# One layer step on one core: TensorE's order in projection, gates and branch products, from a planner's to the program's

## The chip, the cores and the metric

The kernel runs on one core of a Trainium2 chip. The metric is the device time of one execution in microseconds; the kernel before was run three times. TensorE (called PE in the profile) does matrix products and transposes into PSUM; ScalarE (ACT) and VectorE (DVE) read PSUM and do everything elementwise; GpSimd (POOL) does a part of the elementwise work in SBUF; SyncE (SP) issues nearly all DMAs.

## The reference

One inference step of a backbone of two layers over 384 tokens (128 context tokens and 256 latent ones) with 1024 channels. Each layer has a token mixer and an MLP; the change lies in the mixer:

```python
p = _project(h, lp)                        # h @ w_in: inputs of four mixers, and 4 x 1024 gates
o_a = _dense_attention(...)                # A: latent attention, 4 heads
o_b, s_f, s_b = _bi_retention(...)         # B: retention in both directions, 4 heads
o_c = _banded_attention(...)               # C: window and sink, 4 query heads, 2 key heads
o_d = _dense_attention(...)                # D: normalised q and k, 4 query heads, 2 key heads
terms = [jax.nn.sigmoid(gates[..., i * D_MODEL:(i + 1) * D_MODEL]) * (o @ lp['w_branch'][i])
         for i, o in enumerate(outs)]
y = (terms[0] + terms[1] + terms[2] + terms[3]) @ lp['w_o']
x = _layernorm(ALPHA * x + g1 * y, lp['ln1_g'], lp['ln1_b'])
h = x * (1 + sc2) + sh2
f = jnp.square(jax.nn.relu(h @ lp['w_up'])) @ lp['w_down']
x = _layernorm(ALPHA * x + g2 * f, lp['ln2_g'], lp['ln2_b'])
```

## The kernel before

**Precision and products.** Every large product is done as three matmuls: both operands are split into a high and a low part, and high by high, high by low and low by high are summed in PSUM (`mm3`, lines 119 to 122). So lines L120, L121 and L122 are the tile products in all rows; the attention's small matmuls and all transposes have lines of their own (L680 scores, L718 transposes of the softmax, L736 values, L899 transposes of q and k, L809 to L845 branch A's preparation, L965 to L1086 branch B).

**Stages of a layer's mixer.** The projection (lines 1135 to 1142) goes over chunks of columns. A chunk of the kinds a, c, d and b2 gives three tiles, one per block of 128 tokens, each of 24 matmuls with 256 columns (`proj`, L653); a chunk of the kind qk gives two tiles of 24 matmuls with 384 columns (`qk_b`, L945). Layer 0 has six chunks here (16 tiles), layer 1 eight (22 tiles). Then come the four branches in the order A, C, D, B, called br 0, 2, 3, 1 in the code (lines 1193 to 1208). Each has eight gate tiles of 24 matmuls with 384 columns (`gates`, L1148), and after each two gate tiles two branch products of six matmuls with 384 columns each (`products`, L1159), which read a finished branch's output.

**The step.** After each projection or gate tile the program calls `tick()` (L465), and this runs one step of a software pipeline (class `Pipe`, L416). Its 31 tasks, added in lines 1096 to 1122, start one per step, and each task does its next stage in each later step. A task of attention has the stages scores, turn and values (L674, L712, L727): scores are TensorE's product, then the row maximum on VectorE (L689), the negated maximum (L697, or L693 in C), the exponential on ScalarE (L700), the reciprocal (L705) and the scaling (L707 and L708); turn transposes the result; values multiplies it with V. Four such tasks for each of A, C and D alternate between a batch of two query blocks (eight score matmul records) and one of a single block (four). Stages that are marked late (turn) come last in a step. In program order the first scores of A stand in step 6 and their turn in step 7; C's first scores stand in step 14, right behind the transposes of C's last block that they read, and their turn in step 15; C's third batch has its scores in step 18 and its turn in step 19; D's first batch has them in steps 21 and 22. All steps from 1 to 34 have work for TensorE; later ones have none. A step also may take VectorE work of the conditioning's linear map from a list (`ada_v`, L370).

**What sets the order.** The framework traces the program and then a planner orders each engine's instructions by its own estimate of when inputs are ready, with program order as priority. The helper `behind` (L129) adds an edge that fixes the order of two instructions of one engine, without a semaphore; `in_order` (L156) puts such edges between all instructions of the named engines in a block, so that the planner has no choice there. Before, it stands around the first product and around the ends of the two other large products. In `Pipe.step` the helper `held` keeps a step's work behind what was last issued two steps earlier (`HOLD = 2`). In projection, gates and branch products nothing else fixes TensorE's order.

**Buffers that matter.** PSUM has the pools `psa` (three banks: scores take two per batch, and branch products one each), `psg` (two: tiles of projection and gates), `psm` (two: transposes) and `pso` (one). Weights come by SyncE's DMAs into six raw buffers, and ScalarE and VectorE split each into `wh` and `wl` (L281 and L125), four buffers deep.

Of the kernel before, what the change touches and what calls it, by code (L numbers as in the profile page):

```python
# [50 lines left out]
BR_ORDER = (0, 2, 3, 1)  # L51
# [42 lines left out]
def kernel(ctx, tc, a):  # L94
# [14 lines left out]
    def nm(s):  # L109
        counter[0] += 1  # L110
        return f"{s}_{counter[0]}"

    def bank(pool):
        return pool.tile([P, 512], F32, tag="bank", name=nm("bank"))
# [4 lines left out]
    def mm3(out, a_hl, b_hl, start, stop):  # L119
        mm(out, lhsT=a_hl[0], rhs=b_hl[0], start=start, stop=False)  # L120
        mm(out, lhsT=a_hl[0], rhs=b_hl[1], start=False, stop=False)  # L121
        mm(out, lhsT=a_hl[1], rhs=b_hl[0], start=False, stop=stop)  # L122
# [6 lines left out]
    def behind(later, earlier):  # L129
        tc.add_manual_dep(later, earlier.name,  # L130
                          mybir.DependencyInfo(mybir.DependencyClass.NoSync, mybir.DependencyReason.DATA),
                          reason="issue order")
# [22 lines left out]
    @contextmanager  # L155
    def in_order(engines=COMPUTE):  # L156

        pinned.clear()
        n = len(nc.cur_bb.bb.instructions)
        yield  # L160
        for i in nc.cur_bb.bb.instructions[n:]:
            if i.engine in engines and "DMA" not in type(i).__name__:
                if i.engine in pinned:
                    behind(i, pinned[i.engine])
                pinned[i.engine] = i

    def view(hl, pattern, **kw):
        return tuple(t.rearrange(pattern, **kw) for t in hl)
# [57 lines left out]
    def cond_rows(alloc):  # L226
        nc.sync.dma_start(out=csr, in_=a["cond"].partition_broadcast(P))
        for c in range(2):
            for h in range(2):
                x, th = csr[:, c, h * 512:(h + 1) * 512], alloc()  # L230
                nc.scalar.activation(th, x, AF.Tanh, scale=0.5)
                nc.vector.tensor_scalar(out=th, in0=th, scalar1=0.5, scalar2=0.5, op0=ALU.mult, op1=ALU.add)
                nc.vector.tensor_tensor(out=x, in0=x, in1=th, op=ALU.mult)
# [4 lines left out]
    class Stream:  # L238
# [21 lines left out]
        def next(self, splits=SPLITS_AHEAD):  # L260
            i = self.at
            self.at += 1
            self.split(i)
            self.ahead(splits)
            return self.sub[i]
# [19 lines left out]
    def by_k(subs, k):  # L285

        out = []
        for hl in subs:
            v = view(hl, "p (k n) -> p k n", k=k)
            out += [(v[0][:, i], v[1][:, i]) for i in range(k)]  # L290
        return out

    stream = Stream()
    n_f = D_FF // P
    nq = 0
    for l in range(L):
# [14 lines left out]
        for k in range(n_f):  # L311
            f = k + AHEAD if k < n_f - REST else n_f
# [99 lines left out]
    def hk(k):  # L412
        return tuple(h[:, k, :] for h in hT)


    class Pipe:  # L416
# [10 lines left out]
        def step(self):  # L427
            if self.tasks:
                self.live.append(self.tasks.pop(0))
            self.marks.append(last_issued())  # L430
            marks = self.marks[-HOLD - 1] if len(self.marks) > HOLD else {}
            stages = [t.pop(0) for t in self.live if t]
            for late in (False, True):
                for f in stages:
                    if getattr(f, "late", False) == late:
                        with held(marks):
                            f()
            self.live = [t for t in self.live if t]
# [19 lines left out]
    for l in range(L):  # L458
        last = l == L - 1
        pipe = Pipe()  # L460
        p2 = None
# [3 lines left out]
        def tick():  # L465
            pipe.step()
            ticks[0] += 1
            n = 2 if p2 else ([0] + [c for f, c in TICK_OPS if f <= ticks[0]])[-1]
            for _ in range((n + ticks[0] % 2) // 2):
                next(ada_v, None)  # L470
# [130 lines left out]
        at_ctx = tc.tile_pool(name=f"attn{l}", bufs=1, reuse_waits="tile")  # L601
        at = at_ctx.__enter__()

        def t2(name):
            return at.tile([P, 512], F32, tag="t2", name=nm(name), bufs=T2N)
# [22 lines left out]
        def evac_to(key, c0, scale=None):  # L628
            def f(t, b, n=256):
                if (key, t) not in tm:  # L630
                    tm[key, t] = t2("tm" + key)
                x = tm[key, t][:, c0:c0 + n]
                if scale is None:
                    nc.scalar.copy(x, b[:, :n])  # L634
                else:
                    nc.scalar.mul(x, b[:, :n], scale)
            return f

        def proj_part(b, w, n, t, k0, k1):
            for k in range(k0, k1):  # L640
                mm3(b[:, :n], hcol(k, t), w[k], k == 0, k == KT - 1)
# [11 lines left out]
        def proj(w, n, evac, step):  # L653
            for t in range(3):
                b = bank(psg)
                proj_part(b, w, n, t, 0, KT)
                evac(t, b)
                step()
# [286 lines left out]
        def qk_b(i0, scale):  # L945

            def f(w, i):
                if i0 + i == 0:
                    bt["qk"] = at.tile([P, 4, NTOK], F32, tag="kb", name=nm("qkB"))
                b = bank(psg)  # L950
                for k in range(KT):
                    mm3(b[:, :NTOK], tuple(q[:, i * P:(i + 1) * P] for q in w[k]), hk(k), k == 0, k == KT - 1)
                if scale is None:
                    nc.scalar.copy(bt["qk"][:, i0 + i, :], b[:, :NTOK])
                else:
                    nc.scalar.mul(bt["qk"][:, i0 + i, :], b[:, :NTOK], scale)
            return f
# [167 lines left out]
        chunks = [("d", 0, None), ("d", 256, None), ("qk", 0, None), ("qk", 2, 0.125), ("b2", 0, None), ("b2", 256, 0.5)]  # L1125
# [3 lines left out]
        else:  # L1129
            chunks = [("c", 0, None), ("c", 256, None)] + chunks  # L1130
        for t in range(3):
            evac_to("a", 0)(t, banks_a[t], A_W)
        if l == 0:
            cond_rows(lambda: t2("acc"))
        for key, c0, scale in chunks:
            w = by_k([stream.next(), stream.next()], 4)
            if key == "qk":
                for i in range(2):
                    qk_b(c0, scale)(w, i)
                    tick()  # L1140
            else:
                proj(w, 256, evac_to(key, c0, scale), tick)


        acc = [None] * KT
# [2 lines left out]
        def gates(ts_):  # L1148
            for _ in range(2):
                w = view(stream.next(), "p (k n) -> p k n", k=KT)  # L1150
                b = bank(psg)
                for k in range(KT):
                    mm3(b[:, :NTOK], (w[0][:, k], w[1][:, k]), hk(k), k == 0, k == KT - 1)
                tt = t1.tile([P, NTOK], F32, tag="T1", name=nm("tt"), bufs=T1N)
                nc.scalar.activation(tt, b[:, :NTOK], AF.Tanh, scale=0.5)
                ts_.append(tt)
                tick()

        def products(br, c0, ts_, done, hl):  # L1159
            w = view(hl, "p (k n) -> p k n", k=2)  # L1160
            while not o_done[br]:
                tick()
            for i in range(2):
                cc = c0 % 4 + i
                b = bank(psa)
                for k in range(2):
                    mm3(b[:, :NTOK], (w[0][:, k, cc * P:(cc + 1) * P], w[1][:, k, cc * P:(cc + 1) * P]),
                        (o_hl[br][0][:, k], o_hl[br][1][:, k]), k == 0, k == 1)
                done(c0 + i, ts_[i], b[:, :NTOK])
# [20 lines left out]
                                           op1=ALU.subtract)  # L1190
            mT[c] = (mh, ml)

        for n, br in enumerate(BR_ORDER):
            done = (first_done, mid_done, mid_done, last_done)[n]
            for half in range(2):
                if n == 3 and half == 0:
                    while pipe.busy():
                        tick()
                    at_ctx.__exit__(None, None, None)
                    p2_ctx = tc.tile_pool(name=f"p2_{l}", bufs=1, reuse_waits="tile")  # L1200
                    p2 = p2_ctx.__enter__()
                hl = None
                for c0 in (4 * half, 4 * half + 2):
                    ts_ = []
                    gates(ts_)
                    if hl is None:
                        hl = stream.next()
                    products(br, c0, ts_, done, hl)

        def lnc_tile():  # L1210
            return p2.tile([P, D], F32, tag="lnc", name=nm("lnc"), bufs=4)
# [490 lines left out]
```

## Time and profile before

| | us |
|---|---|
| median of 3 runs | 1277.07 |
| lowest and highest | 1276.08, 1277.44 |
| profiled execution, its time | 1276.65 |
| span of its profile | 1274.5 |
| TensorE busy in it | 1253.8 |
| VectorE, ScalarE, GpSimd busy | 854.1, 583.5, 211.2 |

Busy time of TensorE counts a matmul until its modelled end, so consecutive matmuls overlap; what one of a stream costs is the distance between two starts. The rows that the prediction uses come from the page's first part (busy time by engine), from the view by windows (busy time of each engine in chosen stretches) and from the timeline of one engine.

### The profile page before, as it was taken

Reading aid. Unit: us, or ns where it says so; the run is one execution under the profiler, and the core shown is the slowest. Engines: PE = TensorE matmul, PEld = TensorE weight load, DVE = VectorE, ACT = ScalarE, POOL = GpSimd, SP = SyncE. Lnnn points to the kernel's source line nnn. Section 1 sums busy time; section 2 is a strip of 40 time slices with the busy share of each in tenths; the row PEclk is TensorE's granted clock in tenths of the full one; section 3 lists DMA queues with packets and bytes.
Section 4 is the critical chain, followed back from the end, with each engine's and each line's share of the span. In section 5 each row is a group of like instructions: output and inputs, shape, how many; then the busy total and the mean of one; then the engine's idle time right before and its main releaser. Section 6 shows DMA issues by size and latency. Waiting matters only on the chain. (4 is left out here: it accounts for less than half of the span.)

```text
span 1274.5 us, 19089 instructions
## 1 busy us (share of the span) xinstructions
PE 1253.8 (98%) x7246; PEld 1137.6 (89%) x7246; DVE 854.1 (67%) x1537; ACT 583.5 (46%) x1051; POOL 211.2 (17%) x214
## 2 busy tenths in 40 slices
PE   9999999999999999999999999999999999999996
PEld 6789888999989999999898988999998999999995
DVE  4676875899779999343586876597456893333336
ACT  4564564333545444454365566233343744444442
POOL 0031200333232000000061210024221500000003
PEclk9999999999999999999999999999999999999998
DMA  9843323459627887453223422348344263334421
GB/s 366 330 154 118 123 100 104 145 197 337 226 83 246 269 271 273 149 176 140 102 98 133 158 92 83 121 155 322 119 148 162 109 209 132 125 124 159 165 74 50
DMA packets 64827, 211.65 MB, mean 166 GB/s; under 512 B 9248, under 2 KB 13536, under 8 KB 64608
## 3 DMA queue, kind: packets, MB, share of 16 engines
q1 hardware_dynamic: 62016, 201.49, 45.3%
q0 software_dynamic: 2432, 8.42, 2.0%
q8 instruction: 57, 0.93, 0.3%
q10 hardware_dynamic: 288, 0.52, 0.1%
q14 instruction: 34, 0.28, 0.1%
HBM read 206.28 MB, written 4.13 MB: 165 GB/s over the span
## 5 line engine op out<-in xcount | busy, mean ns | idle before, releaser
L125 DVE TENSOR_TENSOR wl<-raw,wh 128x1024 fp32r<-128x1024 f32 (+1 forms) x251 | 317.6, 1270 | 299.4 <-ACT wh L281 298.8
L281 ACT CAST wh<-raw 128x1024 fp32r<-128x1024 f32 x249 | 260.5, 1050 | 447.7 <-PE bank L121 286.9
L120 PE MATMUL bank<-hTh,wh 128*128 128x384 f32 x1040 | 351.4, 338 | 0.0
L122 PE MATMUL bank<-hTh,wl 128*128 128x384 f32 x1040 | 348.8, 336 | 0.6 <-DVE wl L125 0.6
L121 PE MATMUL bank<-hTl,wh 128*128 128x384 f32 x1040 | 348.5, 335 | 0.0
L120 PEld LDWEIGHTS bank<-hTh,wh 128*128 128x128 f32 x1040 | 195.3, 188 | 5.0 <-issue 1.9
L121 PEld LDWEIGHTS bank<-hTl,wh 128*128 128x128 f32 x1040 | 195.3, 188 | 3.2 <-issue 0.9
L122 PEld LDWEIGHTS bank<-hTh,wl 128*128 128x128 f32 x1040 | 195.2, 188 | 1.2 <-DVE wl L125 0.9
L121 PE MATMUL bank<-wl,uh 128*128 128x512 f32 x384 | 150.4, 392 | 0.0
L122 PE MATMUL bank<-wh,ul 128*128 128x512 f32 x384 | 150.3, 392 | 0.0
L120 PE MATMUL bank<-wh,uh 128*128 128x512 f32 x384 | 149.6, 390 | 0.0
L370 DVE CUSTOM_DVE_ANT_0 acc<-raw,csr,bT 128x1024 bf16<-128x1024 f32 x80 | 105.0, 1327 | 1.7 <-POOL rope L756 0.9
L370 DVE CUSTOM_DVE_ANT_0 acc<-lnc,csr,bT 128x1024 bf16<-128x1024 f32 x80 | 100.5, 1293 | 0.0
L1183 POOL TENSOR_TENSOR tt<-tt,tt 128x384 f32<-128x384 f32 x48 | 65.5, 1382 | 205.5 <-DVE tt L1182 205.5
L122 PEld LDWEIGHTS bank<-wh,ul 128*128 128x128 f32 x384 | 71.9, 188 | 15.4 <-DVE ul L125 0.4
L120 PEld LDWEIGHTS bank<-wh,uh 128*128 128x128 f32 x384 | 72.1, 188 | 13.9
L121 PEld LDWEIGHTS bank<-wl,uh 128*128 128x128 f32 x384 | 72.1, 188 | 13.9
L120 PE MATMUL bank<-wh,hTh 128*128 128x256 f32 x240 | 71.7, 299 | 0.2 <-ACT tmc L634 0.2
L122 PE MATMUL bank<-wh,hTl 128*128 128x256 f32 x240 | 68.7, 286 | 0.0
L121 PE MATMUL bank<-wl,hTh 128*128 128x256 f32 x240 | 68.3, 285 | 0.0
L391 POOL DMA_DIRECT2D gd<-gs x4 | 2.4, 595 | 290.4 <-DMA raw<-in_w_u_dram 158.0
L700 ACT ACTIVATE p<-bank,neg 128x384 f32<-128x384 f32 (+1 forms) x72 | 35.8, 508 | 30.1 <-DVE neg L697 16.2
(273 smaller groups left out, 1824.6 us busy)
## 6 DMA issues: line engine op xcount, KB each, us to landing
raw<-in_w_g_dram SPq DMA_DIRECT2D x64, 512.0 KB, 3.5
raw<-in_w_d_dram SPq DMA_DIRECT2D x64, 512.0 KB, 3.5
raw<-in_w_u_dram SPq DMA_DIRECT2D x58, 512.0 KB, 3.6
raw<-in_w_av_dram SPq DMA_DIRECT2D x40, 512.0 KB, 3.9
lnc<-in_w_av_dram SPq DMA_DIRECT2D x40, 512.0 KB, 4.5
raw<-in_w_q_dram SPq DMA_DIRECT2D x28, 512.0 KB, 3.9
raw<-in_w_ada_dram SPq DMA_DIRECT2D x16, 512.0 KB, 8.4
raw<-in_w_b_dram SPq DMA_DIRECT2D x16, 512.0 KB, 3.7
```

The costliest lines, as they stand in the source:

```text
L120: mm(out, lhsT=a_hl[0], rhs=b_hl[0], start=start, stop=False)
L121: mm(out, lhsT=a_hl[0], rhs=b_hl[1], start=False, stop=False)
L122: mm(out, lhsT=a_hl[1], rhs=b_hl[0], start=False, stop=stop)
L125: nc.vector.tensor_tensor(out=low, in0=x, in1=high.bitcast(F32), op=ALU.subtract)
L281: nc.scalar.copy(wh, raw)
L370: nc.vector.tensor_tensor_reduce(out=alloc().bitcast(BF16), in0=w, in1=csr[:, c], scale=1.0, scalar=bT[:, l, u, b:b + 1], op0=ALU.mult, op ...
L391: nc.gpsimd.dma_start(out=g_dram[l][w].rearrange("c (k p) -> (c k) p", p=P), in_=gs)
L700: nc.scalar.activation(p[:, j, c], ss[j][:, c], AF.Exp, bias=neg[:, i, j:j + 1], scale=scale, accum_out=su[:, i, j:j + 1])
L1183: nc.gpsimd.tensor_tensor(out=acc[c], in0=acc[c], in1=t_, op=ALU.add)
```

## The change

TensorE's instructions of the two loops are put between edges of `in_order`, the first block around the projection's chunks, the second around the four branches with gates and products; steps that `tick` runs inside are part of the block. Only TensorE's order is fixed: a tile's 24 matmuls, then all of that step's TensorE work in program order, then the next tile or the branch products. No instruction is added or taken away, and the order of the other engines stays with the planner.

```diff
-        for key, c0, scale in chunks:
-            w = by_k([stream.next(), stream.next()], 4)
-            if key == "qk":
-                for i in range(2):
-                    qk_b(c0, scale)(w, i)
-                    tick()
-            else:
-                proj(w, 256, evac_to(key, c0, scale), tick)
+        with in_order((mybir.EngineType.PE,)):
+            for key, c0, scale in chunks:
+                w = by_k([stream.next(), stream.next()], 4)
+                if key == "qk":
+                    for i in range(2):
+                        qk_b(c0, scale)(w, i)
+                        tick()
+                else:
+                    proj(w, 256, evac_to(key, c0, scale), tick)
...
-        for n, br in enumerate(BR_ORDER):
-            done = (first_done, mid_done, mid_done, last_done)[n]
-            for half in range(2):
...
+        with in_order((mybir.EngineType.PE,)):
+            for n, br in enumerate(BR_ORDER):
+                done = (first_done, mid_done, mid_done, last_done)[n]
+                for half in range(2):
...
+                    for c0 in (4 * half, 4 * half + 2):
+                        ts_ = []
+                        gates(ts_)
+                        if hl is None:
+                            hl = stream.next()
+                        products(br, c0, ts_, done, hl)
```

## Rows read from the trace of the kernel before

**Rows 1.** The page, part 1: busy us, share of the span, instructions by engine.
```profile
PE 1253.8 (98%) x7246; PEld 1137.6 (89%) x7246; DVE 854.1 (67%) x1537; ACT 583.5 (46%) x1051; POOL 211.2 (17%) x214
```

**Rows 2.** Busy time by windows: stretch, length, engines' busy time, granted clock, DMA share, GB/s.
```profile
core 0: us, PE busy (x) PEld busy (x) DVE busy (x) ACT busy (x) POOL busy (x), PEclk, DMA share, GB/s
52.28:265.82 213.54, 209.22 (x1403) 188.38 (x1404) 161.55 (x398) 108.23 (x249) 45.87 (x46) 1.00 0.38 130
265.82:339.05 73.23, 73.19 (x422) 72.72 (x421) 68.02 (x90) 29.36 (x41) 21.97 (x18) 1.00 0.79 277
657.98:856.77 198.79, 196.69 (x1368) 176.37 (x1367) 146.64 (x359) 99.44 (x233) 36.04 (x40) 1.00 0.37 126
...
1262.00:1274.50 12.50, 2.36 (x11) 1.63 (x9) 7.73 (x13) 1.45 (x2) 7.10 (x8) 0.72 0.29 110
```

**Rows 3.** TensorE's timeline in layer 0, step 1: start, us, engine, line, tiles, form, count.
```profile
55.02 0.28 PE L121 MATMUL bank<-wl,hTh 128*128 128x256 f32 x1
55.13 0.28 PE L122 MATMUL bank<-wh,hTl 128*128 128x256 f32 x1
55.26 0.38 PE L789 MATMUL bank<-ident,tma 128*128 128x128 f32 x2
55.39 0.36 PE L120 MATMUL bank<-wh,hTh 128*128 128x256 f32 x1
55.59 0.28 PE L121 MATMUL bank<-wl,hTh 128*128 128x256 f32 x1
```

**Rows 4.** TensorE's timeline in layer 0, C's first scores until their transposes.
```profile
124.40 0.28 PE L121 MATMUL bank<-wl,hTh 128*128 128x256 f32 x1
124.65 1.14 PE L680 MATMUL bank<-qk 64*128 64x384 f32 x8
125.72 0.38 PE L122 MATMUL bank<-wh,hTl 128*128 128x256 f32 x1
125.94 0.28 PE L120 MATMUL bank<-wh,hTh 128*128 128x256 f32 x1
...
132.73 1.09 PE L718 MATMUL bank<-ident,p 128*128 128x128 f32 x8 [0.76 <-ACT p L707]
```

**Rows 5.** Timelines in layer 1: two split batches of scores, and one whole.
```profile
753.11 0.91 PE L680 MATMUL bank<-qk 64*128 64x384 f32 x2
...
754.38 0.91 PE L680 MATMUL bank<-qk 64*128 64x384 f32 x2
...
784.68 0.92 PE L680 MATMUL bank<-qk 64*128 64x384 f32 x4
```

**Rows 6.** Timelines of TensorE and ScalarE: a batch of A, layer 0.
```profile
94.61 2.00 PE L680 MATMUL bank<-kTA,qTA 96*128 96x384 f32 x8
...
100.60 0.91 ACT L707 ACTIVATE p<-p,su 128x384 f32<-128x384 f32 x2 [0.25 <-DVE su L705]
```

**Rows 7.** The same for C's first batch in layer 1.
```profile
728.33 1.14 PE L680 MATMUL bank<-qk 64*128 64x384 f32 x8
...
734.27 0.91 ACT L707 ACTIVATE p<-p,su 128x384 f32<-128x384 f32 x2
```

**Rows 8.** TensorE's timeline around two pairs of branch products, layer 0.
```profile
148.31 0.33 PE L122 MATMUL bank<-o,wl 128*128 128x384 f32 x1
...
150.39 0.45 PE L120 MATMUL bank<-o,wh 128*128 128x384 f32 x1
...
195.28 0.34 PE L120 MATMUL bank<-hTh,wh 128*128 128x384 f32 x1
...
196.84 0.45 PE L120 MATMUL bank<-o,wh 128*128 128x384 f32 x1 [0.35 <-ACT p L700]
```

**Rows 9.** Timelines of TensorE and VectorE, layer 0, step 4.
```profile
71.66 0.27 PE L812 MATMUL bank<-ident,kpe 128*32 128x128 f32 x1
...
72.96 0.29 DVE L815 COPY ckvT<-bank 128x128 f32<-128x128 f32 x1
```

**Rows 10.** TensorE's timeline, layer 0, step 34.
```profile
261.80 0.33 PE L120 MATMUL bank<-o,wh 128*128 128x384 f32 x1
...
264.15 0.41 PE L1086 MATMUL bank<-ident,oB 128*128 128x128 f32 x2 [1.49 <-DVE oB L1078]
```

More of the change, by code (lines that the diff above doesn't have):

```diff
@@ L1191, in last_done @@
             mT[c] = (mh, ml)
-        for n, br in enumerate(BR_ORDER):
-            done = (first_done, mid_done, mid_done, last_done)[n]
-            for half in range(2):
[L1196 to L1208, printed above, removed]
+        with in_order((mybir.EngineType.PE,)):
+            for n, br in enumerate(BR_ORDER):
+                done = (first_done, mid_done, mid_done, last_done)[n]
+                for half in range(2):
+                    if n == 3 and half == 0:
+                        while pipe.busy():
+                            tick()
+                        at_ctx.__exit__(None, None, None)
+                        p2_ctx = tc.tile_pool(name=f"p2_{l}", bufs=1, reuse_waits="tile")
+                        p2 = p2_ctx.__enter__()
+                    hl = None
+                    for c0 in (4 * half, 4 * half + 2):
[4 more added lines that the diff above has]
+                        products(br, c0, ts_, done, hl)
         def lnc_tile():
```

## The prediction

> **What bounds the kernel now.** I read the page's busy times first: TensorE is busy for 1253.8 us, 98% of the span, the next engine for 67% [rows 1]. Then the view by windows, cut at the stretches that the change touches. In layer 0 TensorE's small work (attention, retention, transposes) lies between 52.28 and 265.82, in layer 1 between 657.98 and 856.77; the gate tiles and products behind these stretches are one unbroken run of matmuls before and after (73.23 us with 73.19 busy in layer 0), so the change can do nothing there [rows 2]. In the two stretches TensorE is idle for 213.54 - 209.22 = 4.3 us and 198.79 - 196.69 = 2.1 us [rows 2]. So all waits that a better order could remove come to 6.4 us, 0.5% of the time. VectorE is busy there for 161.55 of 213.54 and 146.64 of 198.79 us, about three quarters [rows 2].
>
> Third, TensorE's timeline over both stretches, laid beside the order that the program would give. In program order each stretch has 35 runs of tile products (34 steps with TensorE work, and the run behind the last). The timeline has 47 in layer 0 and 52 in layer 1. So 12 and 17 times, 29 in all, the planner cut a tile and put a step's work inside it, or a piece of a tile inside a step. The first such cut in layer 0 comes one tile after [rows 3], the last is in [rows 10]. At most of these places TensorE shows no wait at all: the matmuls pulled forward cover one. The change forbids exactly that.
>
> **What it removes.** Every cut costs two changes between kinds of matmul. In a stream of tile products with 256 columns the starts are 0.11 to 0.12 us apart. Around two transposes the way in takes 0.13 and the first matmul behind takes 0.20, an excess of some 0.09 us [rows 3]; around scores it is 0.25 in and 0.22 out, an excess of 0.23 [rows 4]. Most cuts are of both kinds; I take 0.16: 29 x 0.16 = 4.6 us (2.6 to 6.7). Second, scores of two heads that stand together run side by side: four records take 0.92 us whole, but two records take 0.91 when tile products were put between the heads [rows 5]. There are three such splits, all in layer 1: 3 x 0.9 = 2.7 us. Third, the idle 6.4 us go into the new account below, which counts each wait from the start. Removed: 13.7 us (11.7 to 15.8).
>
> **What it adds.** No instruction and no DMA is moved to another queue; SyncE issues the same loads, and weights are split ahead of use (DMA share 0.38 [rows 2]). What is new are waits of TensorE. Matmuls behind a waiting one wait too: the next tile, then its evacuation on ScalarE, then VectorE's use of it. The gap that program order leaves between a producer and its consumer is what TensorE does in between. A tile is 24 x 0.12 = 2.9 us with 256 columns [rows 3] and 24 x 73.23 / 422 = 4.2 us with 384 [rows 2]; a single-block batch of scores takes 0.9 us in C and D [rows 5], and in A some 1.4 us (three quarters of the eight records' 2.00 [rows 6], an estimate).
>
> Softmax. From the end of the scores of a two-block batch to the end of the scaling it takes 100.60 + 0.91 - 96.61 = 4.9 us where VectorE and ScalarE are free [rows 6], with C's mask and sink 734.27 + 0.91 - 729.47 = 5.7 us [rows 7]; in layer 0's first batch of C it was 132.73 - 125.79 = 6.9 us, since weight splits and other work stood ahead on both engines [rows 4]. The turn comes one step later. Step 7: gap 4.2 + 1.4 = 5.6 us in layer 0, 2.9 + 1.4 = 4.3 in layer 1, so waits of 0 to 1.3 and 0.6 to 2.6. Step 9 in layer 1: 0 to 1.5. Step 15, where no scores stand between: gap 2.9 in layer 0 and 4.2 in layer 1, waits 2.8 to 4.0 and 1.5 to 2.7. Step 19 in layer 1 (tile and single-block scores, 3.8): 1.9 to 3.1; in layer 0 products stand between, so nothing. Step 22: 5.1 in layer 0, 3.8 in layer 1: 0 to 1.8 and 1.1 to 3.1. Sum 7.9 to 20.1; I take 12, nearer the free chain, because each wait lets VectorE work off what is queued. The single-block batch of step 17 adds 0 to 3, and I take 1.5.
>
> Banks of branch products. Scores hold two of `psa`'s three banks, so the second product of a pair waits for an exponential or for VectorE's use of the first. The planner put gate matmuls between: the first product ended at 148.5 and the second began at 150.39, 1.9 us; the other pair has 1.56 us between 195.28 and 196.84, of which 0.35 was idle already [rows 8]. In program order these are bare waits. The second pattern stands in both layers: 1.9 + 2 x 1.56 = 5.0. Three more pairs stand behind scores (step 22 in layer 0, step 28 in both), between 0 and 1.56 each; 0.8 each makes 2.4. Sum 7.4 (3.5 to 9.7).
>
> Results needed within the step. Keys of A in step 4 read what the step's own transposes gave, copied by VectorE: 72.96 + 0.29 - 71.66 = 1.6 us, of which 0.29 is the copy [rows 9]; matmuls of the next tile covered it. Others are alike: C's scores in step 14 behind ScalarE's copy, `up_q` in steps 2 and 3 of layer 0, and the third `psm` bank in step 25. Eight places at 0.3 to 1.6; I take 0.8: 6.4 us (2.4 to 12.8).
>
> The last step. Branch B's transposes in step 34 wait for VectorE's L1078. TensorE reached that point at 261.80, did four matmuls of the product and then idled for 1.49, until 264.15 [rows 10]. In program order the whole 2.35 us are bare. Layer 1 has the same; between 0 and 2.35, I take 1.6. Sum 4.0 (2.0 to 4.7).
>
> Sum of waits: 12 + 1.5 + 7.4 + 6.4 + 4.0 = 31.3 us (bounds 15.8 and 50.3). They don't all add, since time lost at one wait brings the other engines closer to the next; I take off 4, an estimate: 27.3. Net: 27.3 - 13.7 = +13.6 us. The profiled execution took 1276.65 us (span 1274.5 and 2.15 around it), 0.4 below the median: 1276.65 + 13.6 = 1290.
>
> **The rivals.**
> First, faster: the other engines follow. They keep the planner's order, and it now knows where TensorE stands. If it put each chain ahead of weight splits and `ada_v`, the turn's waits would be the free chain's, and the others would shrink with them. Then all waits are at their lower bounds, 15.8 less the same 4, and with switches at their dearest 15.8 removed: 1276.65 + 11.8 - 15.8 = 1273. It decides at a sum of waits of 13.7. For it: VectorE has a quarter free [rows 2]. Against it: in step 15 even the free chain (5.7) is longer than the gap (2.9), and the banks' waits hang on the same chain.
>
> Second, the change doesn't do what it says to the time: most runs already stand in program order (35 of 47 and of 52), and waits and switches cancel within 0.2%, about what a measurement of this kernel can tell from no change: 1277.
>
> [...]
>
> **How the numbers follow.** Forecast (1290) 0.64, faster (1273) 0.15, no change (1277) 0.11, clock (1301) 0.10. Slower by over 0.2%: 0.64 + 0.10 = 0.74. The bounds give 1276.65 + 15.8 - 4 - 15.8 = 1273 and 1276.65 + 50.3 - 11.7 = 1315; all waits at their upper bound at once is unlikely, so the range ends at 1304, which takes in the clock's case, and begins at 1274.
>
> **What would show it.** The windows of the two stretches, which end where branch B's last transposes do: longer by some 6 to 8 us each, with idle time of TensorE risen from 6.4 to about 25 us, named by L707, L700 and L1078, the largest in step 15 of layer 0. The tile's runs fall to 35 a stretch, no score batch is split, and the stretch behind keeps its 73.2 us. Wrong if the idle time stays under 13 us, or if the time comes from the stretches that aren't touched.

## The result and the profile after

The changed kernel took 1310.72 us (median of 4 runs, 1309.43 to 1311.59), the kernel before 1276.99: a ratio of 1.0265, 95% interval 1.0252 to 1.0278. It is slower, as forecast, but by 33.7 us where the forecast was 13.6 and the range ended at 1304. The profiled execution took 1309.43 us with a span of 1307.7.

The page of the kernel after, busy us by engine, answers to [rows 1]: TensorE still leads, at 97% in place of 98%.

```profile
span 1307.7 us, 19094 instructions
...
PE 1261.9 (97%) x7246; PEld 1145.5 (88%) x7246; DVE 853.5 (65%) x1537; ACT 583.8 (45%) x1051; POOL 210.3 (16%) x214
```

The windows of [rows 2], cut at the same instructions (from the tile ahead of the first step to the first gate tile behind branch B's last transposes, then the unbroken run of matmuls behind it, for each layer; the columns are length, busy time of each engine, TensorE's granted clock, DMA share, GB/s):

```profile
52.08:287.01 234.93, 215.76 (x1404) 195.84 (x1404) 163.95 (x402) 109.48 (x250) 43.96 (x46) 0.96 0.35 121
287.01:360.34 73.33, 73.11 (x422) 72.79 (x422) 64.44 (x86) 28.37 (x41) 22.80 (x18) 1.00 0.76 271
679.26:890.84 211.58, 198.02 (x1367) 176.64 (x1367) 149.03 (x362) 99.92 (x234) 36.15 (x40) 0.99 0.35 120
890.84:994.90 104.06, 104.06 (x602) 104.06 (x602) 58.82 (x70) 39.06 (x55) 28.00 (x24) 1.00 0.54 192
```

All of the time came in the two stretches: 234.93 - 213.54 = 21.4 us in layer 0 and 211.58 - 198.79 = 12.8 in layer 1; the run behind keeps its 73.3. TensorE's idle time there rose from 6.4 to 19.17 + 13.56 = 32.7 us, by 26.3. Its busy time rose too, from 405.9 to 413.8, by 7.9, though the change was to save some. The other engines did the same work as before.

What TensorE waited for, over the span (engine, tile and line that waited, what released it, us, times, longest):

```profile
PE bank L718 <- ACT p L707: 13.7, 8, 3.8
PE bank L1086 <- DVE oB L1078: 4.1, 2, 2.2
PE bank L120 <- ACT p L700: 3.7, 3, 1.4
PE bank L680 <- ACT qk L900: 2.5, 3, 1.4
PE bank L809 <- DVE sq L790: 2.1, 2, 1.1
PE bank L835 <- DVE ckvT L815: 1.8, 2, 1.4
PE bank L120 <- DVE tt L1180: 1.7, 1, 1.7
...
PE bank L120 <- DVE atts L1018: 1.1, 2, 0.6
```

They are the waits that were forecast, by name and place. (The diff shifts the lines behind it; L1180 is VectorE's first use of a branch product.) The granted clock is the surprise. Before, it was 1.00 in both stretches and 0.72 over the last 12.50 us [rows 2]; now it is 0.50 or 0.51 in five places inside the program, 20.5 us in all:

```profile
136.30:139.70 3.40, 3.40 (x18) 3.40 (x17) 1.24 (x3) 0.81 (x2) 0.00 (x0) 0.50 0.07 19
150.00:156.80 6.80, 5.89 (x21) 5.90 (x22) 0.98 (x2) 1.33 (x3) 0.00 (x0) 0.50 0.38 137
163.60:167.00 3.40, 3.40 (x11) 3.40 (x12) 3.40 (x8) 2.03 (x9) 1.46 (x2) 0.50 0.26 84
283.10:286.50 3.40, 3.39 (x12) 3.40 (x13) 3.40 (x5) 0.64 (x2) 0.00 (x0) 0.50 0.47 166
784.80:788.30 3.50, 3.50 (x19) 3.50 (x18) 3.50 (x7) 2.11 (x8) 2.54 (x2) 0.51 0.40 132
```

Each begins within 1 us of the end of a wait: 3.82 us until 135.53 (step 15), 3.33 until 150.91 (step 17), 1.73 until 163.55 (products behind step 18), 2.19 until 283.11 (step 34) and 1.64 until 784.29 (step 19 of layer 1). TensorE's rows that came behind these waits, with the length of the wait and what ended it in brackets:

```profile
135.53 1.27 PE L718 MATMUL bank<-ident,p 128*128 128x128 f32 x8 [3.82 <-ACT p L707]
...
150.91 1.54 PE L718 MATMUL bank<-ident,p 128*128 128x128 f32 x6 [3.33 <-ACT p L707]
...
163.55 0.66 PE L120 MATMUL bank<-o,wh 128*128 128x384 f32 x1 [1.73 <-DVE tt L1180]
...
283.11 0.66 PE L1086 MATMUL bank<-ident,oB 128*128 128x128 f32 x2 [2.19 <-DVE oB L1078]
...
784.29 1.49 PE L718 MATMUL bank<-ident,p 128*128 128x128 f32 x8 [1.64 <-ACT p L707]
```

### The profile page after: what moved, and what is told of

Read it like the earlier page. It is cut to its first block, busy times and chain, and to the rows that moved or that the text cites. A ratio compares the mean times of both kernels' runs of the same rounds, so it can differ in the third digit from the quotient of the medians.

```text
span 1307.7 us, 19094 instructions
## 1 busy us (share of the span) xinstructions
PE 1261.9 (97%) x7246; PEld 1145.5 (88%) x7246; DVE 853.5 (65%) x1537; ACT 583.8 (45%) x1051; POOL 210.3 (16%) x214
## 5 line engine op out<-in xcount | busy, mean ns | idle before, releaser
L125 DVE TENSOR_TENSOR wl<-raw,wh 128x1024 fp32r<-128x1024 f32 (+1 forms) x251 | 317.1, 1268 | 319.6 <-ACT wh L281 316.8
L370 DVE CUSTOM_DVE_ANT_0 acc<-raw,csr,bT 128x1024 bf16<-128x1024 f32 x80 | 104.8, 1326 | 2.6 <-PE bank L809 1.4
L370 DVE CUSTOM_DVE_ANT_0 acc<-lnc,csr,bT 128x1024 bf16<-128x1024 f32 x80 | 100.4, 1289 | 0.0
L120 PE MATMUL bank<-o,wh 128*128 128x384 f32 x128 | 46.1, 360 | 6.8 <-ACT p L700 3.7
L700 ACT ACTIVATE p<-bank,neg 128x384 f32<-128x384 f32 (+1 forms) x72 | 35.9, 508 | 32.2 <-DVE neg L693 16.3
```

The lines of the kernel that those rows point to most:

```text
L125: nc.vector.tensor_tensor(out=low, in0=x, in1=high.bitcast(F32), op=ALU.subtract)
L370: nc.vector.tensor_tensor_reduce(out=alloc().bitcast(BF16), in0=w, in1=csr[:, c], scale=1.0, scalar=bT[:, l, u, b:b + 1], op0=ALU.mult, op ...
L700: nc.scalar.activation(p[:, j, c], ss[j][:, c], AF.Exp, bias=neg[:, i, j:j + 1], scale=scale, accum_out=su[:, i, j:j + 1])
```

## The experiments

Each kernel of the experiments ran beside the kernel before on the same chip (1275.9 to 1276.7 us). Lengths, idle and busy time are TensorE's, summed over the two stretches, from the same windows as above; "half" is the time at a granted clock of 0.50 or 0.51 in and right behind them.

| kernel | us | ratio, 95% interval | length | idle | busy | half |
|---|---|---|---|---|---|---|
| before | 1276.99 | 1 | 412.3 | 6.4 | 405.9 | 0 |
| after | 1310.72 | 1.0265 [1.0252, 1.0278] | 446.5 | 32.7 | 413.8 | 20.5 |
| projection only | 1295.66 | 1.0152 [1.0135, 1.0169] | 432.9 | 21.0 | 411.9 | 17.1 |
| gates only | 1292.15 | 1.0129 [1.0114, 1.0144] | 426.8 | 19.1 | 407.7 | 3.4 |
| fill | 1308.07 | 1.0250 [1.0235, 1.0266] | 438.7 | 22.0 | 416.7 | 0 |
| turn later | 1293.68 | 1.0136 [1.0121, 1.0152] | 430.3 | 21.8 | 408.6 | 10.2 |
| products first | 1303.95 | 1.0208 [1.0190, 1.0225] | 436.1 | 26.0 | 410.1 | 17.1 |
| both | 1282.58 | 1.0049 [1.0034, 1.0064] | 416.2 | 13.2 | 403.0 | 3.4 |
| short sums | 1296.47 | 1.0159 [1.0138, 1.0180] | 432.8 | 25.9 | 406.9 | 6.8 |
| planner, both | 1275.16 | 0.9982 [0.9970, 0.9995] | 409.2 | 6.3 | 402.9 | 0 |

The three runs with empty steps (1289.98, 1282.33 and 1284.64 us) stand below; two of them shift work across the ends of these windows. Runs that are compared with one another were not all taken side by side; the kernel before differed by up to 1.1 us between their times.

**Half of the change at a time.** Are the waits local, or does lateness from the projection add to the gates' waits? One of the two blocks was taken back, here the second:

```
-        with in_order((mybir.EngineType.PE,)):
+        if True:
             for n, br in enumerate(BR_ORDER):
```

> The program's order stands around the projection tiles alone (steps 1 to 16 in layer 0, 1 to 22 in layer 1); gates and products are the planner's as before. Theory (each wait is local: a producer that is too near to its consumer): the waits that the changed kernel shows in these steps stay, 8.1 us of idle time in layer 0 and 9.1 in layer 1, about 0.24 us more for each of the 14, and the half-level stretches behind step 15 of layer 0 and step 19 of layer 1 (3.4 us each, half of it lost); less some 3 us of switches and of idle time that stood here before: 1277 + 18 = 1295, and together with the run that does the gates alone it comes to the 33.7 us of the whole change within 4. Rival (lateness is carried on: VectorE and ScalarE come out of the first part behind, and the second part pays for it): each part alone costs clearly less than its share, and the two together under 27 us.

> The program's order stands around gate tiles and branch products alone (from step 17 in layer 0, 23 in layer 1). Theory (local waits): 10.9 us of idle time in layer 0 (3.3 of it the turn of step 17) and 4.1 in layer 1, some 2.5 us hidden beside them, and the half-level stretches behind steps 17, 18 and 34 (13.6 us in the changed kernel, half of it lost, 6.8), less some 6 us of switches and idle time that stood there before: 1277 + 17 = 1294. Rival (lateness carried on from the projection): the 3.3 us of step 17 and the fall behind it shrink to nothing, and the run costs under 10 us: below 1287.

Measured: +19.7 us and +16.2 us, together 35.9 against 33.7, near the theory's 18 and 17. The costs of the two halves add, so the waits of one don't come from the other. In the run with the gates alone step 17 still waited 3.4 us, with no pinned projection ahead of it.

**Filling the waits.** What does the clock cost?

```
+        def fill(tb, n):
+            for _ in range(n):
+                mm(tb[:, 0:NTOK], lhsT=hT[0][:, 0, 0:P], rhs=hT[0][:, 0, :], start=True, stop=True)
...
                         tb = bank(psm)
+                        if j == 0 and i == 2:
+                            fill(tb, fills.get((l, ticks[0]), 0))
...
+                if t == 0:
+                    fill(tb, 10)
```

> The changed kernel, with matmuls that nobody uses put into five of its waits, ahead of the transposes of the waiting step and into the same bank: 16 of 384 columns in step 15 and 14 in step 17 of layer 0, 8 each in steps 17 and 19 of layer 1, and 10 ahead of branch B's first transposes in both layers. At some 0.174 us each they take 2.8, 2.4, 1.4 and 1.7 us, less than the waits that they stand in, so that they cost at most 0.2 us a place. Theory (the clock falls because TensorE stood still, and the time at the lower level is lost): the half-level stretches behind these waits go (17 to 20 us of them), and 8 to 10 us with them: 1301 to 1303. Rival (what runs at the lower level hides work of VectorE that TensorE would otherwise wait for): the granted clock is 1.00 again, but idle time rises by as much, and the time stays within 2 us of 1310.7. Second rival (the clock falls for another reason): the clock stays down with the filler in place, and the filler itself takes longer: 1310 to 1314.

Measured: 1308.07 us, 2.7 less than the changed kernel, between the first two theories. The windows of this kernel:

```profile
51.95:280.21 228.26, 215.44 (x1443) 195.27 (x1444) 162.25 (x399) 108.59 (x249) 44.00 (x46) 1.00 0.38 124
677.03:887.45 210.42, 201.23 (x1394) 179.49 (x1393) 148.84 (x362) 100.05 (x234) 36.17 (x40) 1.00 0.37 121
```

The granted clock is 1.00 in both, where the changed kernel has 0.96 and 0.99: with matmuls in these waits it no longer fell there. The 66 filler matmuls take 66 x 73.19 / 422 = 11.4 us [rows 2]; without them TensorE is busy for 405.2 us, against 413.8 in the changed kernel. The lower level had cost 8.6 us of matmul time, and the stretches are 7.8 us shorter. But outside them 4.4 us came back: the profiled run is only 3.4 us shorter in its span. Some 34 to 42 us behind the first stretch ScalarE stood 8.5 us for a weight's load, and a gate tile waited for ScalarE's evacuation (L1166), which stood behind that weight's cast; then TensorE slowed there too: from 325.47 to 328.67 its matmuls start 0.32 us apart, ahead of that and behind it 0.17, and the granted clock is 0.98 over 278 to 353. TensorE's and ScalarE's rows of that place:

```profile
322.45 1.04 ACT L281 CAST wh<-raw 128x1024 fp32r<-128x1024 f32 x1 [8.54 <-DMA raw<-in_w_g_dram]
...
323.94 0.45 PE L120 MATMUL bank<-hTh,wh 128*128 128x384 f32 x1 [1.97 <-ACT tt L1166]
```

What set that load's time was not tried. So the price of the lower level is shown inside the stretches; of the whole time the filler gave back only 2.7 us.

**The turn a step later.** 

```
-                turn.late = True
-
...
-                return scores, turn, values
+                return scores, (lambda: None), turn, values
```

> The changed kernel, with the turn of the probabilities one step later: scores, an empty step, turn, values. Theory (a softmax takes 5 to 7 us and TensorE has 3 to 6 us of its own order in between; a step more gives 3 to 4 us more): the eight waits of L718 on L707, 13.7 us, fall under 3 us, three of the five half-level stretches (behind steps 15, 17 and 19) go with them; some 0.24 us hidden at each place also: 1310.7 - 11 - 2 - 7 = 1290, between 1286 and 1296. Rival (VectorE and ScalarE can't keep up with TensorE in these stretches at all, and a wait that is covered comes back at the next place): L718's waits go, those of products, C's scores and the last step grow, and the time falls by less than 8 us: above 1303.

Measured: 1293.68 us, 17.0 less, inside the theory's range. L718's waits for L707 fell from 13.7 us to 0.5. In layer 0, of this kernel's waits:

```profile
PE bank L120 <- DVE tt L1178: 4.8, 3, 1.9
PE bank L1084 <- DVE oB L1076: 2.2, 1, 2.2
...
PE bank L718 <- ACT p L707: 0.5, 1, 0.5
```

The products' waits stayed and changed their releaser: now VectorE's use of the product holds the bank last.

**Products ahead of the step, and both.** 

```
-                        gates(ts_)
-                        if hl is None:
-                            hl = stream.next()
-                        products(br, c0, ts_, done, hl)
+                        def rest():
+                            if hls[0] is None:
+                                hls[0] = stream.next()
+                            products(br, c0, ts_, done, hls[0])
+
+                        gates(ts_, rest)
```

where `gates` calls `rest()` between the second tile and its step.

> The changed kernel, with each pair of branch products moved ahead of the step in which it stood behind: gate tile, step, gate tile, products, step. A tile of 4.2 us then stands between a step's scores and the products that want their banks, and the products stand ahead of branch B's last transposes in step 34. Theory (local waits): the waits of the products (7.5 us of idle time, five of softmax's banks and two of the retention's) and the two of L1086 (4.1) go, with about 2 us hidden beside them and the half-level stretch behind step 34; against that the batches whose scores stand in steps 18, 22 and 24 lose the products between them and their turn, some 0.5 to 1.5 us each: 1310.7 - 12 = 1299, between 1295 and 1303. Rival (the engines behind are what sets the pace, a covered wait comes back at the next one): less than 6 us: above 1305.

> The later turn and the products ahead of the step, both. The later turn alone took 1293.7 us; what was left there were product waits (7.3 us of idle time) and L1086's (4.1), some 2 us hidden beside them and half of the 7 us at the lower clock. Theory (local waits, that add up): 1293.7 - 14 = 1280, between 1276 and 1284. Rival (they come back): above 1287.

Measured: 1303.95 us alone, just above the theory's 1295 to 1303, and 1282.58 with the later turn, inside its range. Alone, the products' waits are gone, but step 34's fell only from 2.19 to 1.09 us in layer 0, with 1.49 for a weight split (L125) right behind it, and step 19's turn, which lost the products ahead of it, now waits 1.74. The two parts alone save 17.0 and 6.8 us, together 28.1.

**More distance.** One empty step more at four places, with TensorE pinned and, beside it, with the planner's order on every engine; then at the first of these places alone:

```
-        pipe.add(keys_a)
+        pipe.add(lambda: None, keys_a)
...
+            if i == 0:
+                pipe.add(lambda: None)
...
+        pipe.add(lambda: None)
         for i, b in enumerate(bd):
...
-            pipe.add(lambda f=b[0], t=t: (gate_b(t)(), f()), *b[1:])
+            pipe.add(lambda f=b[0], t=t: (gate_b(t)(), f()), *b[1:-1], lambda: None, b[-1])
```

> As the run with both, and one empty step more ahead of the keys of A, of C's first scores, of D's first scores and of branch B's last transposes. Theory (every wait is a distance in the program's order that is too short): the waits on L815 and L900 (4.4 us of idle time in the changed kernel) go too; what is left are up_q in layer 0 (2.0) and odd ones: 1280 - 4 = 1276. Rival (with the order of one engine fixed and the others' not, some 10 us of waits stay wherever the distances are put): above 1282.

> The kernel before (the planner's order on every engine) with the same distances as the run with all of them: later turn, products ahead of the step, the empty steps. It tells what the order alone is worth when the distances are long. Theory A (the planner's cuts only cost where no wait is to be covered; with long distances it still cuts tiles, for some 5 us of changes between kinds of matmul, and saves few waits): within 3 us of the pinned run beside it, about 1275. Theory B (the planner covers what no fixed distance covers): over 4 us faster than the pinned run.

> As the run with both, and one empty step ahead of the keys of A alone. In the run with both, TensorE waited 1.37 us in layer 0 for the copy of L813 and 0.38 and 0.99 in layer 1 at the same place. Theory (a distance of one tile covers a copy, and nothing else is late there): these 2.7 us go, some 0.5 hidden beside them: 1282.6 - 3 = 1279.5. Rival (as with all the empty steps, where C's first softmax came to stand behind D's first norm on VectorE and waited 3.3 us: the planner's order on the other engines changes with each distance, and a new wait comes up): over 1281.5.

Measured: 1289.98 us pinned, 7.4 more than without the empty steps; 1284.64 by the planner; 1282.33 with the keys' step alone, no change. Where TensorE is pinned the rivals held, and by the planner Theory B, but at a time that nobody expected: slower than the kernel before. With the keys' step their 1.37 us in layer 0 went, and 1.04 came at the next transposes (L825). With all the empty steps TensorE waited 3.32 us in step 17 of layer 0, pinned or not, though C's first batch had a step more there. VectorE's timeline in the pinned run, where the scores ended at 129.9:

```profile
131.38 0.56 DVE L872 TENSOR_TENSOR tmd<-sq,ssd 128x384 f32<-128x384 f32 x1 [1.52 <-POOL ssd L188]
131.86 0.55 DVE L865 TENSOR_REDUCE ssd<-sq 128x6 f32<-128x384 f32 x1
132.32 1.28 DVE L370 CUSTOM_DVE_ANT_0 acc<-raw,csr,bT 128x1024 bf16<-128x1024 f32 x1
...
134.42 0.48 DVE L687 TENSOR_TENSOR bank<-bank,cst 128x128 f32<-128x128 f32 x2
```

VectorE first stood for GpSimd in D's first norm, then did the next norm and a sum of the conditioning (L370), and came to the softmax 4.5 us late. The order of the other engines, not TensorE's distance, set that wait. (Behind the last step both runs also waited for weight splits on VectorE, L125: 2.30 us in layer 0 in either, and 2.70 and 1.66 in layer 1.)

**Strangers in the chain.** Strangers are here instructions of other work that stand in an engine's queue between those of a softmax or of another chain that TensorE waits for.

```
-                nc.vector.tensor_tensor_reduce(out=alloc().bitcast(BF16), in0=w, in1=csr[:, c], scale=1.0,
+                m = cols()
+                nc.vector.tensor_tensor_reduce(out=alloc().bitcast(BF16)[:, 0:m], in0=w[:, 0:m], in1=csr[:, c, 0:m], scale=1.0,
```

where `cols()` gives 64 while attention runs and 1024 behind it.

> The changed kernel, with VectorE's sums of the conditioning (L370, 55 of them in the two stretches, 72 us in all) over 64 columns of 1024 while attention runs, which leaves 15 in 16 of each sum out. The planner's order on VectorE put such sums between the instructions of a softmax: 1.3 us each inside the chains of step 17 of layer 0 and of steps 7, 10 and 17 of layer 1. Theory (the chains are longer than the free ones by the strangers in their queue): L718's waits fall from 13.7 us to some 9, the softmax of step 17 in layer 0 from 8.0 us to 6.7, and the time by 5 to 8 us with what the clock gives: 1304. Rival (the planner puts weight splits in their place, or ScalarE and GpSimd set the chain): L718's waits stay over 12.5 us and the time over 1308.

Measured: 1296.47 us, 14.3 less than the changed kernel, far more than expected, and not where expected. L718's waits fell by only 2.0 us, to 11.7: step 17 of layer 0 from 3.33 to 2.56, that of layer 1 not at all (2.21). Step 34's waits, 4.1 us together, vanished, and the half-level time fell from 20.5 to 6.8 us. In the changed kernel three sums stand in branch B's last chain in layer 0, from 274.41, 275.69 and 281.35, the last straight ahead of the product that TensorE waits for:

```profile
279.34 2.09 DVE L1076 TENSOR_SCALAR oB<-oB,mv,rsb 128x64 f32<-128x64 f32 x4
281.35 1.27 DVE L370 CUSTOM_DVE_ANT_0 acc<-raw,csr,bT 128x1024 bf16<-128x1024 f32 x1
...
282.55 0.41 DVE L1078 TENSOR_TENSOR oB<-oB,tmb 128x256 f32<-128x256 f32 x1
```

In step 17 of layer 1 the one that was counted (1.26 us from 770.47) lay beside ScalarE's scaling. Of the saving 6.8 us are idle time of TensorE and 6.9 busy time, the latter with the clock. VectorE also had 46.4 us less to do in the stretches, so the run doesn't tell the place of the sums from their amount.

**The planner with both.** 

> The kernel before (the planner's order on every engine) with the later turn and the products ahead of the step. Beside it stands the same with TensorE pinned, 1282.6 us, whose two stretches hold 13.1 us of idle time, against 6.1 in the kernel before. Theory A (the planner covers most of what is left of the waits, and pays it back in cut tiles): within 4 us of the pinned one, 1279 to 1284. Theory B (where TensorE can pick, the distances were long enough, and it covers without paying as much): 1273 to 1278, as the kernel before. Theory C (the longer distances help the planner as well): below 1273.

Measured: 1275.16 us, 0.9982 of the kernel before [0.9970, 0.9995], Theory B and the lowest of all, though only by some 0.2%. With TensorE pinned the same distances give 1282.58, 7.4 us more, and the idle time accounts for nearly all of it: 13.2 against 6.3 us, with the busy times equal. Windows of the pinned one, then of the planner's:

```profile
51.78:268.72 216.94, 208.35 (x1404) 189.17 (x1404) 161.03 (x396) 107.11 (x248) 44.20 (x46) 1.00 0.40 127
663.95:863.17 199.22, 194.61 (x1367) 175.97 (x1366) 146.51 (x358) 98.78 (x233) 32.69 (x41) 1.00 0.39 125
```

```profile
51.88:264.26 212.38, 208.75 (x1404) 189.85 (x1404) 160.21 (x396) 107.18 (x248) 45.43 (x46) 1.00 0.40 130
658.40:855.22 196.82, 194.20 (x1368) 176.31 (x1366) 146.64 (x359) 98.41 (x233) 32.68 (x40) 1.00 0.39 127
```

## Why the prediction was wrong in size

The mechanism and the sign held. Idle rows over 0.2 us of the changed kernel, sorted by the prediction's terms:

| term | forecast us | measured idle us |
|---|---|---|
| softmax, steps 7 to 22 without 17 | 12 | 8.5 |
| softmax, step 17 | 1.5 | 3.33 + 2.21 = 5.5 |
| banks of the products | 7.4 | 6.6 |
| results needed within the step | 6.4 | 7.5 |
| last step | 4.0 | 4.1 |
| sum | 31.3 | 32.3 |

So the sum of the waits was right within 1 us, and that is partly luck: step 17 took 4.0 us more than its term, the other waits for a softmax 3.5 less. Two lower bounds in it stand below their own terms (3.5 where the banks' terms give 5.0, 2.0 where the last step's give 2.35), so the bound 15.8 is 1.9 us too low, which touches the faster rival's 1273 and the low end of the range alone. Four steps failed.

**The deduction.** "They don't all add" took 4 us off. Between the halves they do: alone they come to 35.9 us of 33.7, and the two cures bring 28.1 where alone they bring 23.8. Whether waits within a half shorten one another is not shown. Against the idle time that was measured this step is some 5 us short (27.3 against 32.3).

**The clock.** The case of that name had a chance of 0.10, at 1301 us. No run shows the 11 us that this puts on top of the forecast; the runs showed 8.6 us of matmul time lost at the lower level (the run with filler). They came beside the forecast's waits and not in their place. The granted clock was 0.50 or 0.51 behind single waits of 1.64 to 3.82 us, and with filler in five of the waits it was 1.00 over both stretches, in place of 0.96 and 0.99.

**The savings.** 7.3 us for 29 switches and three split pairs. The kernels that have the same distances show what a cut costs: pinned, 34 tile runs a stretch; by the planner, 40 and 38; and the ten cuts leave TensorE's busy time the same, 402.97 and 402.95 us. Against the kernel before (47 and 52 runs) both are 3.0 us lower. Each still has one pair of score products in layer 1 kept apart by a wait of 0.2 us (two records alone took 0.91 us, four together 0.92 [rows 5]). So two split pairs are gone, 1.8 us at the prediction's price, and some 1.2 us are left for 20 and 30 cuts fewer. The excess of 0.09 to 0.23 us read around single switches [rows 3, 4] did not add up over the cuts. And one split stayed in the changed kernel: in step 22 of layer 1 the planner is free between the two pinned blocks, so one batch of scores is still split there and that stretch has 37 runs, not 35, a point missed in the diff. This step was 4.3 us too good.

**Step 17.** Its batch has one block, and the prediction put its wait at 0 to 3 us and took 1.5 for both layers, on the notion that fewer blocks make a shorter chain. Layer 1's chain of VectorE and ScalarE, from scores that ended at 766.0:

```profile
766.24 0.29 DVE L687 TENSOR_TENSOR bank<-bank,cst 128x128 f32<-128x128 f32 x1
766.44 0.55 DVE L874 TENSOR_TENSOR tmd<-sq,ssd 128x384 f32<-128x384 f32 x1
...
767.70 0.56 DVE L689 TENSOR_REDUCE mx<-bank 128x1 f32<-128x384 f32 x1
...
768.49 0.17 DVE L693 TENSOR_SCALAR neg<-mx 128x2 f32<-128x2 f32 x1
...
770.13 0.35 DVE L758 TENSOR_TENSOR rope<-tmd,cst 128x192 f32<-128x192 f32 x1
770.40 0.16 DVE L705 RECIPROCAL su<-su 128x2 f32<-128x2 f32 x1
```

```profile
768.69 0.58 ACT L700 ACTIVATE p<-bank,neg 128x384 f32<-128x384 f32 x1 [3.23 <-DVE neg L693]
...
769.91 0.37 ACT L634 COPY tmb<-bank 128x256 f32<-128x256 f32 x1
770.17 0.50 ACT L900 COPY qk<-bank 128x384 f32<-128x384 f32 x1
770.54 0.55 ACT L866 ACTIVATE sq<-tmd 128x384 f32<-128x384 f32 x1
770.96 0.62 ACT L707 ACTIVATE p<-p,su 128x384 f32<-128x384 f32 x1
```

It takes 771.58 - 766.0 = 5.6 us, as long as the free chain of a two-block batch [rows 7]. D's work stands in it on VectorE (L874 and L758) and three instructions of other work (L634, L900, L866) ahead of the scaling on ScalarE. By the starts in these rows they hold it up by some 1.1 us together, an estimate; without them it would take some 4.5, and the gap is a tile and three transposes, 3.4 us. So the strangers are about half of this wait of 2.21 us, and by the same estimate this one-block chain is longer than the gap even without them. In the sum it is made up mostly by step 22, which waited nowhere: behind products in layer 0, unpinned in layer 1.

**The balance.** The stretches grew by 34.2 us and the rest of the span shrank by 1.1. Forecast: idle 27.3 - 6.4 = +20.9, busy -7.3. Measured: +26.3 and +7.9. Of the 15.2 us between the two busy terms 8.6 are the clock, 4.3 savings that weren't there, and 2.3 are left, which no run tells apart.

**The rivals.** That the other engines follow fell: it asked for waits of under 13.7 us, and 32.3 came. They kept the planner's order, and this put strangers into the chains (step 17; C's first batch in the runs with empty steps). That nothing changes fell too. Of the prediction's signs, idle time (25 foretold, 32.7), its releasers, step 15 as the largest wait, 35 runs in layer 0 and the unchanged run behind all came. The stretches were to grow by 6 to 8 us each and grew by 21.4 and 12.8, and no batch was to be split, where one was.

## What to carry to other kernels

Pinning one engine's order here turned the distances between producer and consumer that are shorter than the producer's chain into bare waits (idle time 32.7 us in place of 6.4): sum these waits, take nothing off for overlap without a row that shows it, and price the granted clock beside them, which was 0.50 or 0.51 for 20.5 us of the changed kernel and cost 8.6 us of matmul time. A cut in a stream of matmuls was cheap here (ten of them showed nothing in the busy time, 402.97 and 402.95 us), and a bare wait was not (26.3 us of idle time in a change of 33.7), so check what a planner's cuts cover before taking them away. Longer distances took away most of what the fixed order cost (1282.58 us in place of 1310.72). With the planner left free, the turn a step later and the products ahead of the step came out some 0.2% under the kernel before, which is little; the same distances with a pinned TensorE, and still longer ones, came out slower than it.

## What was not expected of the hardware

The granted clock fell behind some waits and not behind others of the same length. Step 17 of layer 1 waited 2.21 us in the changed kernel and kept a granted clock of 1.00; with products first it waited 2.22 us at the same place, behind the same matmuls at the same pace, and the clock was 0.50 for what followed. With the projection alone the matmuls of the tile behind this step start 0.21 us apart (763.63 to 765.33), in the changed kernel 0.12. First the changed kernel, then the other: the row behind the wait, and a window from just behind its start:

```profile
771.64 1.11 PE L718 MATMUL bank<-ident,p 128*128 128x128 f32 x6 [2.21 <-ACT p L707]
```

```profile
771.80:775.20 3.40, 3.36 (x28) 3.15 (x28) 3.22 (x12) 0.48 (x1) 2.21 (x2) 1.00 0.45 157
```

```profile
771.13 1.45 PE L718 MATMUL bank<-ident,p 128*128 128x128 f32 x6 [2.22 <-ACT p L707]
```

```profile
771.30:774.70 3.40, 3.40 (x17) 3.21 (x17) 2.71 (x12) 0.48 (x1) 2.46 (x2) 0.50 0.48 161
```

Beside six transposes the same length holds 22 matmuls of a tile at the one level and 11 at the other. In the run with filler the clock held (1.00 over the stretch) at the 1.7 us of the products behind step 18, where no filler stood and where it had fallen to 0.50 in the changed kernel. With the gates alone waits of 3.4 us in step 17, 1.7 at these products and 2.2 in step 34 stood as in the changed kernel, and both stretches together hold 3.4 us at the lower level, where the changed kernel has 13.6 behind these three. In these runs the length of a wait by itself didn't decide, and what did was not settled.
